# Gathering x1 instead of its normalised form in a decoder layer's experts, with 1/rms entering at the SiLU

## The chip, the cores and the metric

The kernel runs on one core of one Trainium2 chip. The metric is the time of one execution on the device in microseconds (us), lower is better; where runs are compared, the median of several is taken. A profile comes from one profiled execution with its own time. The engines are TensorE (PE in the rows, PEld for its weight loads), VectorE (DVE), ScalarE (ACT), GpSimd (POOL) and SyncE (SP), which issues nearly all transfers here.

## What is computed

One layer of a decoder: 256 tokens of 1024 columns, fp32. First two token mixers, whose gated sum gives x1 = x + merged @ W_out. Then the part that the change touches, a mixture of 32 experts in 4 groups:

```python
h2 = rmsnorm(x1, norm2_g)            # x1 * r * g, r = 1 / rms of the token's row
g_prob = softmax(h2 @ w_rg + b_rg)   # one group of four
e_logits = (h2 @ w_re + b_re)[group] # two experts of the eight in it
hid = silu(h2 @ w1[e]) * (h2 @ w3[e])
out = x1 + sum over the two experts of weight[e] * (hid @ w2[e])
```

Each expert has w1 and w3 of 1024 x 256 and w2 of 256 x 1024. All 32 are read, 96 MB in all.

## The kernel before

**Tiles.** Tokens lie in two tiles of 128 (t = 0, 1). Weights come in chunks of 1 MB (128 x 2048 fp32): 40 for the mixers and W_out ("wf"), then 96 for the experts ("wm"): 8 groups of 4 experts with 12 chunks each, 8 for w1 and w3 (one per 128 input columns, kc = 0 to 7) and 4 for w2. In what follows a "group" is such a group of four experts.

**What sets the order.** All instructions are written out in one order by hand (`manual_schedule`); no scheduler moves them, and each engine runs its own in that order. Chunks lie in slots of SBUF. `Stream.pump` issues the next chunk's transfer on SP's queue as soon as a slot is free, and `done()` frees one after each kc and after each block of y. SP waits in order: the transfer into a slot is issued when the last matmul that reads the slot's old chunk has ended.

**End of the mixers.** `add_x` adds the last products to x and gives x1 in the tile `acc`, with the sum of squares on ScalarE; `rms2` makes r2 = 1/rms on GpSimd; `x1_T` transposes x1, and `logits` multiplies it by the router's weights into `lg`, one bank per token tile.

**The choice** (`choose`, `choice_end`) is a chain of small VectorE steps for each token tile: lg, mx, mi (the group), pen, le, me, ei (the experts), m1, and Mb, a bf16 mask of the two chosen experts; Mf is the same in fp32. `position` multiplies Mb by a triangle of ones on TensorE (for the second tile by ones with the first tile's mask too) to count each token's place in its expert; `pos_m` is that place, masked by Mf. NCH0, NCH1 and NPOS say how the steps of the two tiles alternate. `sel` compares places with 1 to 32: Sg, a matrix of ones and zeros from tokens to 4 x 32 slots.

**res_init(t, half)** puts x1 into the result's bank by a product with the identity and then has ScalarE scale that half of `acc` by r2 in place; the gather below reads the scaled tile under the name h2. Two calls stand ahead of the choice's end, one within it, the fourth behind the first products of group 0.

**A group.** `gather` multiplies x1's (scaled) columns by Sg into `gp` (half 0: kc 0 to 3, half 1: kc 4 to 7), and VectorE evacuates it with the gain g as `hT`. For group 0, `gather0` and `evac0` do half 0 in parts. `products` runs the eight kc into one bank `h`, then SiLU on ScalarE (L1035), the product `hid` on VectorE (L1036), two transpositions `pt`, and four blocks `y` of the second matmul, each copied to `yy` by ScalarE and added into `res` by `comb` with the combination weights. `mids` says which closures run behind which kc: the second half of the gather, `rest` (the combination weights C and the counts of tokens per expert), `back_a` and `back_b` (the matrix SwT for `comb`), and for the next group `sel` behind kc 4 and its gather behind kc 5 and behind the second y. In the last group, `warm` puts filling matmuls `wps` between the products.

Of the kernel before, what the change touches and what calls it, by code (L numbers as in the profile page):

```python
# [15 lines left out]
P = 128  # L16
# [14 lines left out]
LAG_U = (1, 2, 2)  # L31
NCH0, NCH1, NPOS = 2, 6, (5, 6, 7)
PARK = (5, 7)
# [115 lines left out]
def body(tc, cp, sp, tp, mmp, axp, xT_d, xn_d, wf_d, wm_d, wst_d, bs_d, pv_d, rb_d, wr_d, out_d):  # L149
# [554 lines left out]
    Mb = cp.tile([P, NT, 32], BF16, name="Mb")  # L704
    Mf = cp.tile([P, NT, 32], F32, name="Mf")
    C = cp.tile([P, NT, 32], F32, name="C")
# [70 lines left out]
    def res_init(t, half):  # L777

        c = slice(half * 512, half * 512 + 512)
        res[t][half] = mm_ps(f"res{t}{half}")  # L780
        TE.matmul(res[t][half], ident, A["acc"][:, t, c], start=True, stop=True)
        S.activation(A["acc"][:, t, c], A["acc"][:, t, c], AF.Copy, scale=r2[:, t:t + 1])

# [7 lines left out]
    def choose(t):  # L791
# [13 lines left out]
            lambda: V.scalar_tensor_tensor(Mb[:, t], io32, ei[:, 1:2], m1, ALU.is_equal, ALU.add),  # L805
            lambda: V.scalar_tensor_tensor(Mf[:, t], io32, ei[:, 1:2], m1, ALU.is_equal, ALU.add),
        ]

    def position(t):
        pp = ax_ps(f"pos{t}")  # L810
        for s in range(t):
            TE.matmul(pp[:, :32], ones_b, Mb[:, s], start=s == 0, stop=False)
        TE.matmul(pp[:, :32], utri, Mb[:, t], start=t == 0, stop=True)
        return lambda: V.scalar_tensor_tensor(pos_m[:, t], pp[:, :32], 1.0, Mf[:, t], ALU.add, ALU.mult)

    def weights(t):
# [11 lines left out]
        m2 = t1k([P, 32], f"m2_{t}")  # L828
        V.tensor_tensor(m2, Mf[:, t], m1, ALU.subtract)
        V.tensor_scalar_mul(m2, m2, w[:, 3:4])  # L830
# [87 lines left out]
    logits(1, 1)  # L918
    res_init(0, 0)
    res_init(1, 0)  # L920
    h2 = A["acc"]

    def choice_end(sel, gather0, evac0):
# [4 lines left out]
        for i, f in enumerate(ch[1]):  # L928
            f()
            if i < len(rest0):  # L930
                rest0[i]()
            if i == NPOS[0]:
                pm = position(0)
                res_init(0, 1)
            if i == NPOS[1]:
                pm()
            if i == NPOS[2]:
                sel([0])
        pm = position(1)
        for part in range(2):  # L940
            gather0(0, part)
        pm()
# [20 lines left out]
    def group(g, chunks, done, mid, store):  # L963
# [11 lines left out]
        def gather_mm(ps, i, kc, t, start):  # L975
            TE.matmul(ps[:, i * P:(i + 1) * P], h2[:, t, kc * P:(kc + 1) * P], st["S"][:, t].rearrange("p e s -> p (e s)"),  # L976
                      start=start, stop=t == NT - 1, skip_group_check=True)

        def gather_T(hf):
# [7 lines left out]
        def gather(hf):  # L987
            ps = ax_ps(f"gp{g}{hf}")
            for k in range(4):
                for t in range(NT):  # L990
                    gather_mm(ps, k, hf * 4 + k, t, t == 0)
            gather_T(hf)
            gather_out(hf, ps, range(4))

        def gather0(t, part):
# [24 lines left out]
        def products():  # L1020
# [13 lines left out]
            hid = t1k([P, T], f"hid{g}")  # L1034
            S.activation(hid, ps[:, :256], AF.Silu)  # L1035
            V.tensor_tensor(hid, hid, ps[:, 256:], ALU.mult)  # L1036
            pt = ax_ps(f"pt{g}")
# [49 lines left out]
    def run_groups(next_, done_, first, final):  # L1087
# [5 lines left out]
        else:  # L1093
            sel()
            gather(0)
        mids[0][0] = [lambda: res_init(1, 1)] if first else []
        mids[0][1] = [lambda: gather(1)]
        mids[0][2] = [first] if first else []
        mids[0][3] = [back_a]
        mids[0][6] = [back_b]  # L1100
        for g in range(NGRP):
            if g + 1 < NGRP:
                sel_, gather_, back_a_, back_b_ = gr[g + 1][:4]
                mids[g][4] = [sel_]
                mids[g][5] = [lambda ga=gather_: ga(0)]
# [114 lines left out]
```

## Time and profile before

| | before |
|---|---|
| time, median of 3 runs | 468.51 us (467.79 to 469.26) |
| profiled execution: time, span | 468.38 us, 466.7 us |
| TensorE busy | 438.9 us (94% of the span) |
| TensorE weight loads | 334.8 us (72%) |
| VectorE, ScalarE, GpSimd busy | 207.4, 175.3, 94.7 us |
| transfers | 148.80 MB, mean 319 GB/s |
| chain that ended last | PE 81%, DMA 7%, DVE 3%, ACT 3% |

The span runs from the first to the last instruction; the time has some 1.7 us around it. "Busy" is an average over stages with different limits, so it does not say which engine a stage waits for. The chain that ended last is followed back from the last instruction, at each step to what released it, or to the instruction before it on its engine; a share of it is work that the end can be traced to, which need not be work whose removal would move the end. The page's row of transfers by slices of the span shows stretches with little traffic in the mixers and one near the start of the experts' part; behind that it reads 9 tenths and more in each slice but the last.

### The profile page before, as it was taken

How to read it: one execution, taken by the hardware profiler on the slowest of the kernel's cores; microseconds unless marked ns; L12 is line 12 of the kernel's file. 1: busy time of each engine (PE TensorE's matmuls, PEld its weight loads, DVE VectorE, ACT ScalarE, POOL GpSimd, SP SyncE). 2: the span in 40 equal slices, each digit the busy share in tenths (PEclk: the TensorE clock that was granted, in tenths of full speed). 3: DMA queues.
4: the chain of work that ended last, by engine and by line, in shares of the span. 5: the costliest groups of instructions: out<-in, count | busy, mean ns of one | idle time of the engine just before them, and what ended most of it. 6: DMA issues, size and time to landing. Idle time of an engine off the chain costs nothing.

```text
span 466.7 us, 8463 instructions
## 1 busy us (share of the span) xinstructions
PE 438.9 (94%) x3446; PEld 334.8 (72%) x3446; DVE 207.4 (44%) x389; ACT 175.3 (38%) x332; POOL 94.7 (20%) x118
## 2 busy tenths in 40 slices
PE   8989999999999999999999996989898989889984
PEld 6768778878999999999998842645545554636542
DVE  4676576778797655555774643111111011110012
ACT  5747657665665655533444341111000010101001
POOL 1057296456568100004000100000000000000000
PEclk9999999999999999999999998999999999999998
DMA  7999992550227887598767889999999999999992
GB/s 244 344 425 421 416 402 105 180 179 2 93 91 268 322 312 271 213 364 302 310 239 303 315 326 407 422 418 421 406 418 420 421 418 413 412 421 419 422 382 88
DMA packets 27453, 148.80 MB, mean 319 GB/s; under 512 B 3216, under 2 KB 6032, under 8 KB 11152
## 3 DMA queue, kind: packets, MB, share of 16 engines
q1 hardware_dynamic: 27264, 148.18, 80.3%
q8 instruction: 29, 0.48, 0.4%
q14 instruction: 16, 0.13, 0.1%
q10 hardware_dynamic: 144, 0.02, 0.0%
HBM read 147.14 MB, written 1.05 MB: 318 GB/s over the span
## 4 chain that ended last, share of the span: by engine, by line
PE 81%; DMA 7%; DVE 3%; ACT 3%; issue 2%; POOL 1%; SPq 1%; ACTq 0%
PE h L1025 10%; PE y L1067 7%; PE gp L976 6%; PE res L1046 6%; DMA w<-in_wm_dram 4%; DMA xn<-in_xn_dram 2%; PE v L355 2%; PE u L384 2%; PE ga L386 2%; PE b L386 2%; PE b L385 2%; PE b L384 2%; PE a L386 2%; PE a L385 2%; PE a L384 2%
## 5 line engine op out<-in xcount | busy, mean ns | idle before, releaser
L343 DVE TENSOR_TENSOR hl<-w,hl 128x1024 fp32r<-128x1024 f32 (+2 forms) x88 | 90.8, 1036 | 63.3 <-ACT hl L339 61.0
L339 ACT CAST hl<-w 128x1024 fp32r<-128x1024 f32 (+1 forms) x88 | 84.6, 968 | 83.9 <-PE a L386 12.8
L1025 PE MATMUL h<-w,hT 128*32 128x512 f32 x512 | 61.6, 598 | 0.5 <-DMA w<-in_wm_dram 0.4
L984 DVE TENSOR_TENSOR hT<-gp,pv 128x512 f32<-128x512 f32 (+1 forms) x19 | 11.3, 606 | 98.5 <-PE gp L976 98.5
L345 POOL TENSOR_TENSOR hl<-w,hl 128x352 fp32r<-128x352 f32 x32 | 40.5, 1275 | 21.8 <-ACT hl L339 21.7
L1067 PE MATMUL y<-w,hidT 128*32 128x256 f32 (+1 forms) x528 | 34.1, 389 | 4.9 <-issue 4.4
L1073 ACT COPY yy<-y 128x256 f32<-128x256 f32 (+1 forms) x33 | 12.1, 366 | 69.7 <-PE y L1067 69.7
L976 PEld LDWEIGHTS gp<-Sg,acc 128*128 128x128 f32 x256 | 30.4, 192 | 9.2 <-issue 8.0
L1011 POOL TENSOR_TENSOR Sw<-Sg,C 128x128 f32<-128x128 f32 x16 | 6.1, 399 | 151.4 <-PE res L1046 137.0
L1046 PE MATMUL res<-yy,SwT 128*128 128x128 f32 (+1 forms) x192 | 34.8, 323 | 1.1 <-ACT yy L1073 1.0
L1046 PEld LDWEIGHTS res<-yy,SwT 128*128 128x128 f32 x192 | 25.9, 190 | 12.0 <-issue 6.4
L976 PE MATMUL gp<-Sg,acc 128*128 128x128 f32 x256 | 32.0, 278 | 2.1 <-DVE Sg L972 2.1
L1025 PEld LDWEIGHTS h<-w,hT 128*32 128x32 f32 x512 | 13.4, 109 | 24.6 <-issue 19.2
L1067 PEld LDWEIGHTS y<-w,hidT 128*32 128x32 f32 x528 | 16.1, 112 | 17.1 <-issue 9.7
L1035 ACT ACTIVATE hid<-h 128x256 f32<-128x256 f32 x8 | 3.1, 383 | 54.8 <-PE h L1025 54.8
L1036 DVE TENSOR_TENSOR hid<-hid,h 128x256 f32<-128x256 f32 x8 | 3.4, 421 | 35.1 <-ACT hid L1035 35.1
L215 PEld LDWEIGHTS <-ones_b 128*128 128x128 bf16 x205 | 13.2, 106 | 7.8 <-issue 6.7
L384 PE MATMUL u<-xh,hl 128*128 128x256 f32 x64 | 18.8, 293 | 0.0
L384 PE MATMUL ga<-xh,hl 128*128 128x256 f32 x64 | 18.2, 284 | 0.0
L386 PE MATMUL ga<-xh,hl 128*128 128x256 f32 x64 | 18.1, 283 | 0.0
L385 PE MATMUL ga<-xl,hl 128*128 128x256 f32 x64 | 18.1, 283 | 0.0
L384 PE MATMUL gb<-xh,hl 128*128 128x256 f32 x64 | 18.1, 283 | 0.0
(219 smaller groups left out, 957.3 us busy)
## 6 DMA issues: line engine op xcount, KB each, us to landing
w<-in_wm_dram SPq DMA_DIRECT2D x89, 1024.0 KB, 12.6
w<-in_wf_dram SPq DMA_DIRECT2D x36, 1024.0 KB, 11.6
w<-in_wm_dram SPq DMA_DIRECT2D x24, 256.0 KB, 9.1
w<-in_wf_dram SPq DMA_DIRECT2D x8, 256.0 KB, 4.9
w<-in_wf_dram SPq DMA_DIRECT2D x4, 512.0 KB, 8.2
xT<-in_xT_dram SPq DMA_DIRECT2D x8, 128.0 KB, 4.9
xn<-in_xn_dram SPq DMA_DIRECT2D x1, 1024.0 KB, 8.7
xs<-in_xn_dram SPq DMA_DIRECT2D x1, 1024.0 KB, 9.4
```

The lines of the kernel that those rows point to most:

```text
L215: TE.matmul(wps[:, :P], ones_b, ones_b, start=True, stop=True)
L339: S.copy(hl[:, 0, c], raw[:, c])
L343: V.tensor_tensor(hl[:, 1, c.start:m], raw[:, c.start:m], hl[:, 0, c.start:m].bitcast(F32), ALU.subtract)
L345: G.tensor_tensor(hl[:, 1, m:c.stop], raw[:, m:c.stop], hl[:, 0, m:c.stop].bitcast(F32), ALU.subtract)
L384: TE.matmul(o, wh, ah[:, kc], start=kc == 0, stop=False)
L385: TE.matmul(o, wh, al[:, kc], start=False, stop=False)
L386: TE.matmul(o, wl, ah[:, kc], start=False, stop=kc == KC - 1)
L976: TE.matmul(ps[:, i * P:(i + 1) * P], h2[:, t, kc * P:(kc + 1) * P], st["S"][:, t].rearrange("p e s -> p (e s)"), start=start, stop=t == N ...
L1025: TE.matmul(ps[e * SL:(e + 1) * SL], st["h"][kc // 4][:, kc % 4, e * SL:(e + 1) * SL], piece(w, e), start=kc == 0, stop=kc == KC - 1)
L1046: TE.matmul(res[t][c // 512][:, c % 512:c % 512 + n], st["SwT"][:, t * P:(t + 1) * P], yy[:, o:o + n], start=False, stop=True, skip_group_ ...
L1067: TE.matmul(py[e * SL:(e + 1) * SL, :n], hidT[:, f, e * SL:(e + 1) * SL], w[e][:, f], start=f == 0, stop=f == 1)
L1073: S.copy(yy, py[:, :n])
```

## The change

x1 itself is gathered; 1/rms of the tokens is gathered by a product of its own into the slots (`slot_r2`, behind the second half of each group's gather) and enters as ScalarE's scale of the SiLU and in the product of `hid`. `res_init` loses ScalarE's scaling, and all four calls stand behind kc 4 of group 0. Mf goes; Mb is read in its place. NCH1 and NPOS change how the steps of the choice alternate, and the first tile's gather is divided around the second position. In group 0 the second half of the gather moves from behind kc 1 to behind kc 2, and `rest` from behind kc 2 to behind kc 3.

```diff
-NCH0, NCH1, NPOS = 2, 6, (5, 6, 7)
+NCH0, NCH1, NPOS = 2, 8, (1, 3, 4)
...
     def res_init(t, half):
-        c = slice(half * 512, half * 512 + 512)
         res[t][half] = mm_ps(f"res{t}{half}")
-        TE.matmul(res[t][half], ident, A["acc"][:, t, c], start=True, stop=True)
-        S.activation(A["acc"][:, t, c], A["acc"][:, t, c], AF.Copy, scale=r2[:, t:t + 1])
+        TE.matmul(res[t][half], ident, A["acc"][:, t, half * 512:half * 512 + 512], start=True, stop=True)
...
             lambda: V.scalar_tensor_tensor(Mb[:, t], io32, ei[:, 1:2], m1, ALU.is_equal, ALU.add),
-            lambda: V.scalar_tensor_tensor(Mf[:, t], io32, ei[:, 1:2], m1, ALU.is_equal, ALU.add),
...
-        return lambda: V.scalar_tensor_tensor(pos_m[:, t], pp[:, :32], 1.0, Mf[:, t], ALU.add, ALU.mult)
+        return lambda: V.scalar_tensor_tensor(pos_m[:, t], pp[:, :32], 1.0, Mb[:, t], ALU.add, ALU.mult)
...
-    res_init(0, 0)
-    res_init(1, 0)
-    h2 = A["acc"]
+    x1 = A["acc"]
...
             if i == NPOS[0]:
                 pm = position(0)
-                res_init(0, 1)
             if i == NPOS[1]:
                 pm()
             if i == NPOS[2]:
                 sel([0])
+        gather0(0, 0)
         pm = position(1)
-        for part in range(2):
-            gather0(0, part)
+        gather0(0, 1)
         pm()
         sel([1])
...
+        def slot_r2():
+
+            ps = ax_ps(f"r2s{g}")
+            for t in range(NT):
+                TE.matmul(ps[:, :1], st["S"][:, t].rearrange("p e s -> p (e s)"), r2[:, t:t + 1], start=t == 0, stop=t == NT - 1)
+            st["r2"] = tp.tile([P, 1], F32, tag="r2s", name=f"r2s{g}", bufs=2)
+            V.tensor_copy(st["r2"], ps[:, :1])
...
             gather_out(hf, ps, range(4))
+            if hf == 1:
+                slot_r2()
...
-            S.activation(hid, ps[:, :256], AF.Silu)
-            V.tensor_tensor(hid, hid, ps[:, 256:], ALU.mult)
+            S.activation(hid, ps[:, :256], AF.Silu, scale=st["r2"])
+            V.scalar_tensor_tensor(hid, ps[:, 256:], st["r2"], hid, ALU.mult, ALU.mult)
...
-        mids[0][0] = [lambda: res_init(1, 1)] if first else []
-        mids[0][1] = [lambda: gather(1)]
-        mids[0][2] = [first] if first else []
-        mids[0][3] = [back_a]
+        mids[0][2] = [lambda: gather(1)]
+        mids[0][3] = [first, back_a] if first else [back_a]
...
-                mids[g][4] = [sel_]
+                mids[g][4] = [sel_] + [lambda t=t, hf=hf: res_init(t, hf) for t in range(NT) for hf in range(2) if first and g == 0]
```

TensorE between the router's logits and the first products, before (res is the result's bank, the digits behind it the token tile and the half; gp000 and gp001 are the two parts of group 0's gather; ident_152 is the identity):

```order
L781 MATMUL res00_2902<-acc_75_2750,ident_152 128x512
L781 MATMUL res10_2905<-acc_75_2750,ident_152 128x512
L813 LDWEIGHTS utri_168
L813 MATMUL pos0_2923<-Mb_182,utri_168 128x32
L781 MATMUL res01_2925<-acc_75_2750,ident_152 128x512
L812 LDWEIGHTS ones_b_111
L812 MATMUL pos1_2935<-Mb_182,ones_b_111 128x32
L813 LDWEIGHTS utri_168
L813 MATMUL pos1_2935<-Mb_182,utri_168 128x32
L976 MATMUL gp000_2938<-Sg0_2931,acc_75_2750 128x128 x2
L976 MATMUL gp001_2941<-Sg0_2931,acc_75_2750 128x128 x2
```

The same place now:

```order
L809 LDWEIGHTS utri_168
L809 MATMUL pos0_2911<-Mb_182,utri_168 128x32
L969 MATMUL gp000_2923<-Sg0_2917,acc_75_2749 128x128 x2
L808 LDWEIGHTS ones_b_111
L808 MATMUL pos1_2926<-Mb_182,ones_b_111 128x32
L809 LDWEIGHTS utri_168
L809 MATMUL pos1_2926<-Mb_182,utri_168 128x32
L969 MATMUL gp001_2929<-Sg0_2917,acc_75_2749 128x128 x2
```

The three passes with the identity are gone from here, and the first tile's part gp000 stands ahead of the second tile's position.

TensorE behind kc 3 of group 0, before (h0 is the products' bank with the chunk w that each kc reads, gp10 the first half of group 1's gather, pw0 the transposition in `back_b`):

```order
L1025 MATMUL h0_2959<-w_59_2124,hT01_2984 32x512 x4
L1025 MATMUL h0_2959<-w_60_2155,hT01_2984 32x512 x4
L976 MATMUL gp10_3054<-Sg1_3045,acc_75_2750 128x128 x8
L1025 MATMUL h0_2959<-w_61_2215,hT01_2984 32x512 x4
L1016 MATMUL pw0_3071<-ident_152,Sw0_3036 128x128 x2
```

The same place now:

```order
L1028 MATMUL h0_2947<-w_59_2123,hT01_2975 32x512 x4
L779 MATMUL res00_3038<-acc_75_2749,ident_152 128x512
L779 MATMUL res01_3040<-acc_75_2749,ident_152 128x512
L779 MATMUL res10_3042<-acc_75_2749,ident_152 128x512
L779 MATMUL res11_3044<-acc_75_2749,ident_152 128x512
L1028 MATMUL h0_2947<-w_60_2154,hT01_2975 32x512 x4
L969 MATMUL gp10_3052<-Sg1_3035,acc_75_2749 128x128 x8
L1028 MATMUL h0_2947<-w_61_2214,hT01_2975 32x512 x4
```

All four passes stand between kc 4 and kc 5.

VectorE in the choice, before (the digit behind a name is the token tile; Mb, Mf and pos_m hold both tiles):

```order
L796 SCALAR_TENSOR_TENSOR lg1_2875<-lg1_2893,r2_180,rb_2226 128x40
L803 MAX_INDEX ei0_2873<-me0_2872,le_0_2871 128x8
L797 MAX mx1_2876<-lg1_2875 128x8
L804 TENSOR_SCALAR m10_2874<-io32_169,ei0_2873 128x32
L798 MAX_INDEX mi1_2877<-mx1_2876,lg1_2875 128x8
L805 SCALAR_TENSOR_TENSOR Mb_182<-io32_169,ei0_2873,m10_2874 128x32
L799 TENSOR_SCALAR pen1_2878<-io32_169,mi1_2877 128x4
L806 SCALAR_TENSOR_TENSOR Mf_183<-io32_169,ei0_2873,m10_2874 128x32
L800 TENSOR_TENSOR le_1_2879<-lg1_2875,pen1_2878 128x32
L802 MAX me1_2880<-le_1_2879 128x8
```

The same place now:

```order
L800 MAX_INDEX ei0_2872<-me0_2871,le_0_2870 128x8
L801 TENSOR_SCALAR m10_2873<-io32_169,ei0_2872 128x32
L793 SCALAR_TENSOR_TENSOR lg1_2874<-lg1_2892,r2_180,rb_2225 128x40
L802 SCALAR_TENSOR_TENSOR Mb_182<-io32_169,ei0_2872,m10_2873 128x32
L794 MAX mx1_2875<-lg1_2874 128x8
L795 MAX_INDEX mi1_2876<-mx1_2875,lg1_2874 128x8
L796 TENSOR_SCALAR pen1_2877<-io32_169,mi1_2876 128x4
L810 SCALAR_TENSOR_TENSOR pos_m_181<-pos0_2911,Mb_182 128x32
L797 TENSOR_TENSOR le_1_2878<-lg1_2874,pen1_2877 128x32
L965 TENSOR_TENSOR Sg0_2917<-io32p_170,pos_m_181 128x128
L799 MAX me1_2879<-le_1_2878 128x8
```

Tile 0's ei and m stand ahead of tile 1's lg, Mf is gone, and tile 0's place and selection stand further ahead among tile 1's steps.

## Rows read from the trace of the kernel before

**Rows 1.** Chain that ended last, in order of time: start, length, what.

```profile
426.12 20.48 DMA w<-in_wm_dram
```

**Rows 2.** Instructions in order of time, last group: start, length, engine, line [idle before].

```profile
444.16 1.06 PE L1025 MATMUL h<-w,hT 128*32 128x512 f32 x8 [0.19 <-DMA w<-in_wm_dram]
...
446.64 1.07 PE L1025 MATMUL h<-w,hT 128*32 128x512 f32 x8 [0.19 <-DMA w<-in_wm_dram]
...
448.19 0.42 DVE L1036 TENSOR_TENSOR hid<-hid,h 128x256 f32<-128x256 f32 x1 [22.27 <-ACT hid L1035]
449.33 0.39 PE L1039 MATMUL pt<-ident,hid 128*128 128x128 f32 x2
```

**Rows 3.** Busy time by stretch: five engines, then granted clock, DMA share, GB/s.

```profile
272.50:275.00 2.50, 2.50 (x15) 0.60 (x12) 0.00 (x0) 0.96 (x2) 0.00 (x0) 1.00 0.53 156
275.00:446.50 171.50, 156.98 (x1516) 88.60 (x1516) 22.96 (x63) 19.56 (x51) 6.09 (x16) 0.99 1.01 417
```

**Rows 4.** SP's issues of expert chunks in order of time: start, length, count.

```profile
264.50 2.61 SPq L121 DMA_DIRECT2D w<-in_wm_dram  x4
...
272.93 0.33 SPq L123 DMA_DIRECT2D w<-in_wm_dram  x1
...
302.04 0.33 SPq L123 DMA_DIRECT2D w<-in_wm_dram  x1
```

**Rows 5.** The chain that ended last again, from the router to group 1.

```profile
261.20 0.82 PE lg L789 x8
...
267.08 1.79 PE res L781 x4
268.89 0.95 PE res L781 x2
269.99 1.88 PE gp L976 x16
...
272.87 1.05 PE res L781 x2
...
289.85 3.25 PE y L1067 x32
...
312.70 1.93 PE y L1067 x32
```

**Rows 6.** VectorE in order of time, the choice of the second token tile.

```profile
267.19 0.26 DVE L796 SCALAR_TENSOR_TENSOR lg<-lg,r,rb 128x40 f32<-128x40 f32 x1 [0.54 <-PE lg L789]
...
269.51 0.24 DVE L805 SCALAR_TENSOR_TENSOR Mb<-io,ei,m 128x32 bf16<-128x32 f32 x1
...
270.26 0.29 DVE L972 TENSOR_TENSOR Sg<-io32p,pos_m 128x128 f32<-128x128 f32 x1
```

**Rows 7.** All engines in order of time, group 0.

```profile
276.94 0.69 DVE L984 TENSOR_TENSOR hT<-gp,pv 128x512 f32<-128x512 f32 x1 [4.55 <-PE gp L976]
...
277.98 2.78 PE L1025 MATMUL h<-w,hT 128*32 128x512 f32 x24
...
282.39 0.48 DVE L972 TENSOR_TENSOR Sg<-io32p,pos_m 128x128 f32<-128x128 f32 x2
282.82 2.02 PE L976 MATMUL gp<-Sg,acc 128*128 128x128 f32 x16 [2.06 <-DVE Sg L972]
...
288.87 0.46 PE L1039 MATMUL pt<-ident,hid 128*128 128x128 f32 x2 [1.67 <-DVE hid L1036]
```

**Rows 8.** Busy time by stretch, group 0's y and the like place of group 1.

```profile
289.00:292.50 3.50, 2.98 (x30) 1.34 (x34) 0.42 (x1) 0.37 (x1) 0.00 (x0) 0.52 1.03 431
...
310.00:314.00 4.00, 2.35 (x35) 1.17 (x31) 0.85 (x2) 0.55 (x2) 0.00 (x0) 1.00 1.02 424
```

**Rows 9.** ScalarE's groups of instructions by shape: count, busy us, mean ns.

```profile
L448 ACT ACTIVATE qT<-pt_q,gqk 128x512 f32<-128x512 f32 x4 | 2.5, 678 | 0.0
...
L450 ACT COPY kT<-pt_k 128x512 f32<-128x512 f32 x4 | 2.1, 581 | 0.0
```

**Rows 10.** The same view of VectorE.

```profile
L468 DVE SCALAR_TENSOR_TENSOR sc<-dist,sc 128x384 f32<-128x384 f32 x16 | 8.1, 544 | 0.0
```

More of the change, by code (lines that the diff above doesn't have):

```diff
@@ L704, in body @@
     Mb = cp.tile([P, NT, 32], BF16, name="Mb")
-    Mf = cp.tile([P, NT, 32], F32, name="Mf")
     C = cp.tile([P, NT, 32], F32, name="C")
@@ L828, in weights @@
         m2 = t1k([P, 32], f"m2_{t}")
-        V.tensor_tensor(m2, Mf[:, t], m1, ALU.subtract)
+        V.tensor_tensor(m2, Mb[:, t], m1, ALU.subtract)
         V.tensor_scalar_mul(m2, m2, w[:, 3:4])
@@ L975, in gather_mm @@
         def gather_mm(ps, i, kc, t, start):
-            TE.matmul(ps[:, i * P:(i + 1) * P], h2[:, t, kc * P:(kc + 1) * P], st["S"][:, t].rearrange("p e s -> p (e s)"),
+            TE.matmul(ps[:, i * P:(i + 1) * P], x1[:, t, kc * P:(kc + 1) * P], st["S"][:, t].rearrange("p e s -> p (e s)"),
                       start=start, stop=t == NT - 1, skip_group_check=True)
+        def slot_r2():
[4 more added lines that the diff above has]
+            V.tensor_copy(st["r2"], ps[:, :1])
         def gather_T(hf):
```

## The prediction

> **What bounds the kernel now.** I read the end first, then walk back to the place that decides it. The page's chain is four fifths TensorE, but the chain in order of time holds one stretch of 20.48 us, from 426.12 to 446.60, in which the weight transfers came last [rows 1]. Ahead of it the chain only says that TensorE was busy; behind it stands a fixed tail. So the question is since when the transfers run without a gap. The table by stretch answers it: from 275 us to 446.5 the DMA share is 1.01, at 417 GB/s; between 272.5 and 275 it is 0.53 [rows 3]. The queue had run dry because no slot was free: SP issued nothing from 264.50 + 2.61 = 267.11 to 272.93 [rows 4], and then one chunk of 1 MB as soon as the first products of group 0 had read theirs (271.87 to 272.87) [rows 5]. From that issue to a full queue it takes 275.0 - 272.93 = 2.1 us. In the last group the products start 2.48 us apart (444.16, 446.64), one chunk each, the second behind a wait for its transfer [rows 2]. So the end of the kernel is **the first slot that group 0 frees, plus a fixed number of chunks at 2.48 us, plus the tail**.
>
> One more condition: a later slot must not come so late that the queue runs dry again. Counting the issue at 272.93 as the first, the n-th has to come by 272.93 + (n - 1) x 2.48. The thirteenth, the first of group 1, came at 302.04 and was needed by 302.69: 0.65 us to spare [rows 4]. It is the tight one, since eight slots of a group come from its products, four from its y, and all of group 0's work stands ahead of it. What delays group 0 by more than 0.65 us costs time.
>
> **The change, part by part.** *The way to the first products.* Three of the four passes that put x1 into the result stood ahead of them: 1.79 us for two and 0.95 for the third [rows 5]. They lie beside VectorE's choice, though: Mb of the second token tile ends at 269.51 + 0.24 = 269.75 whatever TensorE does, and its position and its selection (270.26 to 270.55) follow from it [rows 6]. Before, the whole gather stood behind that Mb, from 269.99 to 271.87: 0.94 for the first tile, 0.94 for the second [rows 5]. Now half of the first tile's part stands ahead of it, so 0.47 less follows. On VectorE, ei and m of tile 0 now run before lg of tile 1, in what was an idle stretch of 0.54 us [rows 6], and Mf is gone; they partly filled waits between dependent steps, so the gain there lies between 0 and the 0.54; I take 0.15, nearer to nothing, since each step of tile 1 still waits for the one before. Then the second selection ends at 270.40, the first tile's last quarter at 269.99 - 0.15 + 0.47 = 270.31, and the second tile's half runs from 270.40 to 271.34 instead of ending at 271.87: **0.5 us sooner**, between 0.4 (nothing from VectorE: 270.55 + 0.94 = 271.49) and 0.9 (all of it). The gather's wait for ScalarE's scaled x1 goes too; it stood beside Mb and is in this sum. The first issue moves to 272.43.
>
> *Group 0.* All four passes now stand behind its fifth products: 1.79 + 0.95 + 1.05 = 3.79 us, of which 1.05 was in the group already, so +2.74 [rows 5]. The new product that gathers 1/rms by slot is two fp32 matmuls with one moving column. The nearest row is the router's logits, four with 40 columns in 0.82 us [rows 5]: 0.41 us, an upper end; nothing at all, as under the loads beside it, is the lower. I take the upper one. In exchange TensorE's wait of 2.06 us for the second group's selection is covered: between the gather's second half and the second group's gather stand 0.41 of the new product, three products at 2.78 / 3 = 0.93 and the 3.79, together 7.0 us. VectorE needs 5.93 from the start of the evacuation (276.94) to the selection's end (282.87), and the new copy of one column, 0.2 [rows 7]; 0.9 us of cover are left. Sum to the eighth products' end: -0.5 + 2.74 + 0.41 - 2.06 = **+0.6 us**. The sixth and seventh slots are freed later, too, but the seventh, tightest of them, is still in time (the products behind the second group's gather: 282.82 + 2.02 + 1.0 = 285.8 before [rows 7], so 286.4; needed by 272.43 + 14.88 = 287.3). By the thirteenth issue group 1's new product adds 0.41: **+1.0**. The order of the queue's issues is the same as before, and no transfer is added; ScalarE loses four scalings for whose end no one waits later, and its table load for Exp moves up into idle time: nothing.
>
> *The clock.* In the stretch 289 to 292.5 the granted clock was 0.52, the lower of its two levels (1.2 and not 2.4 GHz) for most of it [rows 8], after TensorE had been idle for 2.06 us and then for 1.67 [rows 7]. The first two blocks of y took 3.25 us in it; two blocks of the next group take 1.93 [rows 5]. So 1.3 us of group 0's length hang on that fall. With the 2.06 us filled I take the clock to stay, as it does at the like place of the next group (310 to 314: 1.00) [rows 8]: the thirteenth issue is then 1.0 - 1.3 = -0.3 us against before, and no slot is late.
>
> The Trainium skill (TensorE: Matmul & The Clock Gate, "Why this matters for your kernels") says that a pause between bursts of matmuls can bring the clock down and that dense work holds it up; by that rule the fall goes with the filled pause, and the sum stays the forecast's. The rule speaks as well of the pause of 1.67 us, which stays: if that one is enough, the fall comes back and the second case below holds. No row here shows which of the two pauses brought it.
>
> *All groups.* ScalarE's SiLU takes a column as its scale: evacuations of 512 columns take 678 ns with one and 581 without, so +0.10; VectorE's product becomes a scalar-tensor-tensor, which takes 544 ns for 384 columns, so between 0.36 (by length) and 0.54 for 256 against 0.42 now: -0.06 to +0.12 [rows 2, 9, 10]. In the last group, where it would count, hid is ready at 448.19 + 0.42 = 448.61 and its transposition starts at 449.33, behind TensorE's filling matmuls [rows 2]: 0.72 us of cover for at most 0.22. Without the cover it costs 0.04 to 0.22. Seven more times 0.41 us on TensorE lie under the transfers.
>
> **The rivals.** (a) Forecast: the stream starts 0.5 us sooner and stays fed. The profiled execution took 468.38 us (span 466.7), 0.13 under the median of 468.51; the same step from the median gives **468.0**.
> (b) The clock falls again: then the thirteenth issue is 1.0 us later with 0.65 to spare; the gain is used up and the end moves by +0.35: 468.9. For it: the pause before the transposition stays. Against: the idle 2.06 us ahead of it are gone.
> (c) Slower: VectorE's chain for the combination weights, now behind the evacuation and the new copy, ends later than TensorE's cover, and the wait of 2.06 us stays beside the passes moved in, the clock falling as before. The thirteenth issue is then 1.0 + 2.06 = 3.1 late, the queue dry for 3.1 - 0.65 = 2.4: 470.9. It decides from a delay of 2.1 us (0.65 to spare plus 1.4). Against it: 0.9 us of cover left over.
> (d) The chain's own price: the passes were what the first products waited for, and all 1.79 + 0.95 = 2.74 us come off: 465.8. For it: the chain names TensorE there. Against: VectorE's steps, which end at 270.55 by themselves.
> (e) TensorE decides the end, and the new products cost 7 x 0.41 = 2.9 on it against the 0.5: 470.9. Against: the 20.48 us in which it waited for transfers.
>
> **How the numbers follow.** Chances: (a) 0.60, (b) 0.23, (c) 0.05, (d) 0.06, (e) 0.03, and 0.03 that the start moves without any effect (468.5). A difference of 0.3%, 1.4 us, is about what a measurement of this kernel can tell from no change; (a), (b) and the last lie within it. So faster by more 0.07 ((d) and a little of (a) with a run's spread), within 0.85, slower 0.08. The range: (a) with its ends 0.4 and 0.9 is 467.6 to 468.1, (b) ends at 468.9; the runs shown (467.79 to 469.26) spread by about 0.7 to each side, of which I add 0.6 below and 0.5 above for a median: 467.0 to 469.4. That holds (a), (b) and the case without effect, 0.86, and leaves out (c), (d) and (e).
>
> **What would show it.** Right: SP's first issue of group 0 near 272.4; the DMA share full from 274.5; no idle TensorE before the second group's gather; the clock at 1.00 through 289 to 293; the thirteenth issue before 302.2; the last group's products again every 2.48 us with 0.5 us less in front. Wrong: a DMA share under 0.9 between 290 and 304 is (b) or (c), by whether the clock or the wait for the selection stands in front of it; a first issue before 271 is (d); no wait for transfers before the last group is (e).

## The result and the profile after

The changed kernel takes 475.5 us (median of 4 runs, 474.5 to 479.1) where the kernel before, run beside it, takes 468.65: a ratio of 1.0158, with a 95% interval of 1.0119 to 1.0196. It is **slower by 7 us**; the prediction said 468.0 with 467.0 to 469.4. The profiled execution took 475.41 us with a span of 473.7, against 468.38 and 466.7 before.

The front of the program, up to the router, is the same but for a shift: the choice of the second token tile starts on VectorE at 266.55, 0.64 us sooner than in [rows 6]. I start from there. VectorE's steps in order of time, after:

```profile
266.55 0.26 DVE L793 SCALAR_TENSOR_TENSOR lg<-lg,r,rb 128x40 f32<-128x40 f32 x1
...
268.78 0.25 DVE L802 SCALAR_TENSOR_TENSOR Mb<-io,ei,m 128x32 bf16<-128x32 f32 x1
...
269.53 0.29 DVE L965 TENSOR_TENSOR Sg<-io32p,pos_m 128x128 f32<-128x128 f32 x1
```

From lg to the start of the second selection (Sg) it takes 2.98 us, against 270.26 - 267.19 = 3.07 before [rows 6]. So VectorE's part became a little shorter, as was forecast (0.15). TensorE in order of time, the same place (in brackets its idle time and what ended it):

```profile
267.02 0.18 PE L809 MATMUL pos<-Mb,utri 128*128 128x32 bf16 x1 [0.58 <-DVE Mb L802]
268.21 0.68 PE L969 MATMUL gp<-Sg,acc 128*128 128x128 f32 x4 [1.02 <-DVE me L799]
...
269.09 0.18 PE L809 MATMUL pos<-Mb,utri 128*128 128x32 bf16 x1 [0.17 <-DVE Mb L802]
269.11 2.84 PE L969 MATMUL gp<-Sg,acc 128*128 128x128 f32 x12
271.88 2.48 PE L1028 MATMUL h<-w,hT 128*32 128x512 f32 x16
```

The passes over x1 that had stood here are gone, and nothing fills their place: TensorE waits 0.58 and 1.02 us. Behind these waits twelve products of the gather and 16 of the first hidden products take 2.84 and 2.48 us. The clock is down, as a table by stretch shows (busy time of five engines with counts, then granted clock, DMA share and GB/s):

```profile
270.00:272.00 2.00, 2.00 (x12) 1.78 (x16) 0.50 (x3) 0.00 (x0) 0.00 (x0) 0.50 0.83 291
272.50:275.00 2.50, 2.50 (x24) 0.56 (x16) 0.00 (x0) 0.00 (x0) 0.00 (x0) 0.89 0.28 40
275.00:446.50 171.50, 158.37 (x1448) 90.57 (x1445) 23.89 (x71) 19.16 (x50) 6.12 (x16) 0.97 1.01 417
446.50:452.00 5.50, 5.50 (x79) 3.62 (x76) 0.00 (x0) 0.00 (x0) 0.00 (x0) 1.00 1.00 410
289.00:292.50 3.50, 1.51 (x22) 0.88 (x26) 0.91 (x2) 0.89 (x2) 0.00 (x0) 1.00 0.99 393
313.50:317.50 4.00, 4.00 (x34) 2.36 (x35) 0.00 (x0) 0.74 (x2) 0.00 (x0) 0.57 1.01 424
...
384.00:388.00 4.00, 3.53 (x43) 2.69 (x44) 0.37 (x1) 0.74 (x2) 0.30 (x1) 1.00 1.02 424
```

The first line is the half clock, 0.50 from 270 to 272 (1.2 and not 2.4 GHz). The second has a clock of 0.89 and a DMA share of 0.28 where before had 1.00 and 0.53 [rows 3]: the queue stays dry longer. SP's issues in order of time give the same:

```profile
265.50 1.51 SPq L121 DMA_DIRECT2D w<-in_wm_dram  x1
273.57 1.19 SPq L123 DMA_DIRECT2D w<-in_wm_dram  x2
```

The first issue of group 0 is at 273.57, 7.02 us behind lg, against 272.93 and 5.74 before [rows 4, 6]: 1.28 us later where I had written 0.5 sooner. All that the earlier front gave (0.64) is lost, and 0.64 more.

Group 0 itself, in order of time, all engines:

```profile
277.04 0.50 PE L976 MATMUL r2s<-r,Sg 128*128 128x1 f32 x4
...
279.61 3.70 PE L779 MATMUL res<-acc,ident 128*128 128x512 f32 x8
...
282.75 0.48 DVE L965 TENSOR_TENSOR Sg<-io32p,pos_m 128x128 f32<-128x128 f32 x2
...
284.24 2.05 PE L969 MATMUL gp<-Sg,acc 128*128 128x128 f32 x16
...
290.48 0.44 PE L1042 MATMUL pt<-ident,hid 128*128 128x128 f32 x2 [1.83 <-DVE hid L1039]
```

The gather for group 1 no longer waits for its selection (the 2.06 us of [rows 7] are gone), and the clock is 1.00 from 289 to 292.5 where it was 0.52 [rows 8]. Up to here the forecast holds but for its start. What follows is what it did not see. The chain that ended last, the two blocks of y at the head of the groups, where before had 1.93 in group 1 [rows 5]:

```profile
291.43 1.93 PE y L1070 x32
...
313.46 3.15 PE y L1070 x32
...
337.13 2.93 PE y L1070 x32
...
360.80 2.71 PE y L1070 x32
...
384.47 1.93 PE y L1070 x32
```

In groups 1, 2 and 3 they run at half clock (0.57 over the four microseconds from 313.5 in the table), and the products on res behind them are slow, too: 1.65 us for each of the three. Ahead of each of them TensorE stands and waits for hid. That pause after, in group 1:

```profile
311.34 0.47 ACT L1038 ACTIVATE hid<-h,r2s 128x256 f32<-128x256 f32 x1 [7.06 <-PE h L1028]
311.85 0.48 DVE L1039 SCALAR_TENSOR_TENSOR hid<-h,r2s,hid 128x256 f32<-128x256 f32 x1 [1.75 <-ACT hid L1038]
312.39 0.44 PE L1042 MATMUL pt<-ident,hid 128*128 128x128 f32 x2 [1.17 <-DVE hid L1039]
```

and the same place of the kernel before:

```profile
310.74 0.38 ACT L1035 ACTIVATE hid<-h 128x256 f32<-128x256 f32 x1 [7.07 <-PE h L1025]
311.16 0.42 DVE L1036 TENSOR_TENSOR hid<-hid,h 128x256 f32<-128x256 f32 x1 [1.67 <-ACT hid L1035]
311.63 0.44 PE L1039 MATMUL pt<-ident,hid 128*128 128x128 f32 x2 [1.02 <-DVE hid L1036]
```

SiLU takes 0.47 instead of 0.38 and the multiplication 0.48 instead of 0.42, so that TensorE's pause is 1.17 instead of 1.02.

Last, the end of the chunks. TensorE in order of time, last group, after:

```profile
438.62 1.06 PE L1028 MATMUL h<-w,hT 128*32 128x512 f32 x8
439.62 1.29 PE L215 MATMUL wps<-ones_b 128*128 128x128 bf16 x20
440.84 1.07 PE L1028 MATMUL h<-w,hT 128*32 128x512 f32 x8
...
452.16 1.06 PE L1028 MATMUL h<-w,hT 128*32 128x512 f32 x8
...
454.38 1.07 PE L1028 MATMUL h<-w,hT 128*32 128x512 f32 x8
```

and of the kernel before:

```profile
430.17 1.06 PE L1025 MATMUL h<-w,hT 128*32 128x512 f32 x8
431.16 1.29 PE L215 MATMUL wps<-ones_b 128*128 128x128 bf16 x20
432.38 1.06 PE L1025 MATMUL h<-w,hT 128*32 128x512 f32 x8
...
439.27 1.06 PE L1025 MATMUL h<-w,hT 128*32 128x512 f32 x8
...
441.68 1.07 PE L1025 MATMUL h<-w,hT 128*32 128x512 f32 x8
```

After, every product of the last group follows the one ahead by 2.22 us (452.16 to 454.38), but for one step of 2.44 with two transpositions in it, and no row has a wait for a transfer. 2.22 us is TensorE's own pace: one product (1.0) and the 20 fill products behind it (1.2). Before, the first ones also follow at 2.22 (430.17 to 432.38; 2.45 with the transpositions); only the last three come later than that, by steps of 2.41 (439.27 to 441.68), 2.48 and 2.48, the last two with a wait of 0.19 us for a transfer [rows 2]. So **TensorE paced nearly the whole of the kernel before**, and had some 0.7 us to spare at its end (0.19 + 0.26 + 0.26), not a stretch of 20 us.

The 7 us then add up. The last group's first product is at 438.62 instead of 430.17, +8.45. Of that +0.60 was there at the start of group 1 (301.52 against 300.92). Between them lie six groups of 22.03 instead of 21.54 us, +2.94 (0.34 for the new products of 1/rms, 0.15 for the pause), and three falls of the clock at 1.65, +4.9. 0.7 us of it fill TensorE's spare time: the last product is later by 454.38 - 446.64 = 7.7. Behind it the tail is 0.7 shorter than before (473.7 - 454.38 = 19.3 against 20.1); what remains is 7.0. These 0.7 are no gain of the change: the engines' work in the tail is the same, and the stretch behind the last evacuation, 5.6 here and 6.4 before, lies anywhere between 5.6 and 7.0 in the profiles of the kernels below.

### The profile page after: what moved, and what is told of

Its sections match the earlier page's. It is cut to its first block, busy times and chain, and to the rows that moved or that the text cites. A ratio compares the mean times of both kernels' runs of the same rounds, so it can differ in the third digit from the quotient of the medians.

```text
span 473.7 us, 8518 instructions
## 1 busy us (share of the span) xinstructions
PE 447.2 (94%) x3478; PEld 342.2 (72%) x3478; DVE 209.8 (44%) x395; ACT 173.1 (37%) x328; POOL 92.8 (20%) x118
## 4 chain that ended last, share of the span: by engine, by line
PE 87%; DMA 3%; DVE 2%; ACT 2%; issue 2%; POOL 1%; SPq 1%; ACTq 0%
PE h L1028 12%; PE res L1049 7%; PE y L1070 7%; PE gp L969 6%; PE wps L215 2%; DMA xn<-in_xn_dram 2%; PE v L355 2%; PE u L384 2%; PE b L386 2%; PE b L385 2%; PE b L384 2%; PE a L386 2%; PE a L385 2%; PE a L384 2%; PE gb L386 2%
## 5 line engine op out<-in xcount | busy, mean ns | idle before, releaser
L343 DVE TENSOR_TENSOR hl<-w,hl 128x1024 fp32r<-128x1024 f32 (+2 forms) x88 | 91.9, 1048 | 60.8 <-ACT hl L339 60.2
L1070 PE MATMUL y<-w,hidT 128*32 128x256 f32 (+1 forms) x528 | 35.8, 403 | 4.9 <-issue 4.4
L1049 PE MATMUL res<-yy,SwT 128*128 128x128 f32 (+1 forms) x192 | 36.8, 335 | 1.1 <-ACT yy L1076 1.0
L1049 PEld LDWEIGHTS res<-yy,SwT 128*128 128x128 f32 x192 | 27.2, 198 | 13.5 <-issue 8.4
L969 PE MATMUL gp<-Sg,acc 128*128 128x128 f32 x256 | 33.5, 284 | 1.1 <-DVE me L799 1.0
L1038 ACT ACTIVATE hid<-h,r2s 128x256 f32<-128x256 f32 x8 | 3.8, 474 | 54.1 <-PE h L1028 54.0
L1039 DVE SCALAR_TENSOR_TENSOR hid<-h,r2s,hid 128x256 f32<-128x256 f32 x8 | 3.9, 484 | 35.3 <-ACT hid L1038 35.3
L384 PE MATMUL ga<-xh,hl 128*128 128x256 f32 x64 | 18.2, 284 | 0.0
L384 PE MATMUL gb<-xh,hl 128*128 128x256 f32 x64 | 18.1, 283 | 0.0
L385 PE MATMUL gb<-xl,hl 128*128 128x256 f32 x64 | 18.1, 283 | 0.0
L386 PE MATMUL gb<-xh,hl 128*128 128x256 f32 x64 | 18.1, 283 | 0.0
```

The lines of the kernel that those rows point to most:

```text
L343: V.tensor_tensor(hl[:, 1, c.start:m], raw[:, c.start:m], hl[:, 0, c.start:m].bitcast(F32), ALU.subtract)
L384: TE.matmul(o, wh, ah[:, kc], start=kc == 0, stop=False)
L385: TE.matmul(o, wh, al[:, kc], start=False, stop=False)
L386: TE.matmul(o, wl, ah[:, kc], start=False, stop=kc == KC - 1)
L969: TE.matmul(ps[:, i * P:(i + 1) * P], x1[:, t, kc * P:(kc + 1) * P], st["S"][:, t].rearrange("p e s -> p (e s)"), start=start, stop=t == N ...
L1049: TE.matmul(res[t][c // 512][:, c % 512:c % 512 + n], st["SwT"][:, t * P:(t + 1) * P], yy[:, o:o + n], start=False, stop=True, skip_group_ ...
```

## The experiments

Theory T: TensorE sets the pace, so its work counts in every group. The products of 1/rms cost their length; the columns on SiLU and multiplication cost the clock by a longer pause; the emptied choice costs one more fall of the clock. Rivals S, by run: the moved pieces themselves; something else than the clock behind the columns; the transfers, as the prediction had it. The kernel before took 468.55 us beside the first four runs, 468.71 beside the next four and 467.94 beside the last four.

**Each part alone, on the kernel before.** The products of 1/rms with their copy, unused:

```diff
+            if hf == 1:
+                slot_r2()
```

> The kernel before with the product that gathers 1/rms by slot and its copy added behind each gather's second half; the result is not used. Theory T: seven such products of 0.34 to 0.5 us stand on TensorE ahead of the last group, 2.4 to 3.0 us, of which 0.7 are to spare: 470.3 to 471.0. The prediction's step (they lie under the transfers): 468.6.

Measured: 470.83 us, ratio 1.0038 (0.9994 to 1.0082). The last group's eight products all stand at TensorE's pace now:

```profile
447.54 1.06 PE L1035 MATMUL h<-w,hT 128*32 128x512 f32 x8
449.76 1.06 PE L1035 MATMUL h<-w,hT 128*32 128x512 f32 x8
```

The group takes 21.89 us (311.43 to 333.32 between two transpositions; 21.88 in the next), +0.34; seven times that is 2.4, less 0.7 to spare is 1.7. The span of the profiled execution (470.1) is 3.4 us longer than before (466.7): it has one fall of the clock beside the products, at 357, in a group of 23.87 us, 2.0 more than its neighbours; its groups began 0.7 sooner (first product at 271.10 instead of 271.80); and its tail is 0.3 longer. The prediction's step (nothing, "under the transfers") would have been 468.6. The interval just reaches 1, so the time alone leaves it at "probably"; the pace in the trace is plain.

The column, as one of ones, which changes no value:

```diff
+    one = cp.tile([P, 1], F32, name="one")
+    G.memset(one, 1.0)
...
-            S.activation(hid, ps[:, :256], AF.Silu)
-            V.tensor_tensor(hid, hid, ps[:, 256:], ALU.mult)
+            S.activation(hid, ps[:, :256], AF.Silu, scale=one)
+            V.scalar_tensor_tensor(hid, ps[:, 256:], one, hid, ALU.mult, ALU.mult)
```

> The kernel before with a column of ones as the scale of the SiLU and in the product of hid (scalar-tensor-tensor instead of tensor-tensor); everything else as before. Theory T with the pause as the cause of the falls: each group's pause grows by 0.15 us (1.17 instead of 1.02), by itself 7 x 0.15 - 0.7 = +0.35 us, and the clock falls behind some of the pauses in groups 1 to 6, 1.65 us each: 470 to 475. Theory T with another cause of the falls (the new product, or where group 0 ends): 468.9 and no fall in groups 1 to 6. Rival S: 468.6.

Measured: 473.97 us, ratio 1.0134 (1.0105 to 1.0163). The pause is 1.18, and the chain shows three falls of the clock:

```profile
334.06 1.93 PE y L1069 x32
355.76 2.75 PE y L1069 x32
...
400.80 3.40 PE y L1069 x32
424.14 2.86 PE y L1069 x32
```

A column on two small instructions, 0.15 us of pause a group or 1 us in all, costs 5.4 us (5.3 in the span, 472.0): 1.0 and three times 1.65, less 0.7 to spare, is 5.2. The rest of this execution cancels: group 0 lacks the fall that it has before (1.2 less), the groups began 0.7 later, and the tail is 0.7 longer. To see whether it is the clock, 14 fill products in the pause of each group, on this same kernel:

```diff
-            if store:
-                warm(NW[1])
+            warm(NW[1] if store else 14)
```

> The kernel before with a column of ones as the SiLU's scale and in the multiplication (474.0 without the fill), and 14 fill products in each pause. Theory T (the column's price of 5 us is the clock, which falls behind a pause of 1.17 instead of 1.02 us): no half clock from group 1 on, 468.0 to 469.6. Rival S (the longer pause itself or ScalarE and VectorE behind it cost it): 471 or more.

Measured: 468.04 us, ratio 1.0007 (0.9981 to 1.0033). No group from 1 on falls, and the whole price is gone, with the column still there. So the column's price is the clock.

The third part, order and late passes without the other two, as an edit of the changed kernel (1/rms is left out of the experts, so its values are not those of the layer):

```diff
-            if hf == 1:
-                slot_r2()
...
-            S.activation(hid, ps[:, :256], AF.Silu, scale=st["r2"])
-            V.scalar_tensor_tensor(hid, ps[:, 256:], st["r2"], hid, ALU.mult, ALU.mult)
+            S.activation(hid, ps[:, :256], AF.Silu)
+            V.tensor_tensor(hid, hid, ps[:, 256:], ALU.mult)
```

> The changed kernel without the four r2 products per group and with SiLU and the multiplication as they were before (1/rms is left out of the experts' branch): what is left of the change is the order of the choice, x1 itself in the gather, and the sums' start in group 0's middle. Theory T (TensorE paces the groups, the longer pause before the transposition and the r2 products cost about 7 us between groups 0 and 7, the clock's fall in the choice costs about 1.3 us of TensorE): group period back at 21.5, no half clock in groups 1 to 6, the pause back at 1.02; group 7 starts 0.4 to 1.0 us later than in the kernel before, and the time is 468.4 to 469.9, taken 469.2. Rival S (the moved pieces themselves, that is the order of the choice or the late start of the sums, cost most of the 7 us): above 473. The prediction's own step (stream 0.5 us sooner and nothing else): 467.9.

Measured: 468.72 us, ratio 0.9997 (0.9973 to 1.0022). The clock falls in the choice as in the changed kernel, at 271, the first slot is 7.16 us behind lg, the pauses are back at 1.02 and no group falls. So the reordering can't be told from nothing in the end (the interval is some 1.2 us to each side), and the two things that carry 1/rms cost the 7 us.

**The changed kernel with its pauses filled** (14 products, the same edit as above):

> The changed kernel with 14 small filling matmuls (0.065 us each, 0.9 us in all) on TensorE in the pause between each group's last products and the transposition of hid; nothing else differs. Theory T (TensorE paces the end of the kernel, with about 0.7 us to spare, and in groups 1 to 3 the clock falls behind this pause, 1.65 us each): the falls in groups 1 to 3 go and with them 4.9 us of 475.5, so about 470.6. Rival S (the weight stream decides the end, as I predicted, and it was late or ran dry): TensorE's pace in groups 1 to 6 is of no matter, so 475.5 as before, even where the clock stays.

Measured: 470.67 us, ratio 1.0052 (1.0022 to 1.0082). The pause is down to 0.28, and y runs at full clock in all groups; group 2:

```profile
333.98 0.44 PE L1041 MATMUL pt<-ident,hid 128*128 128x128 f32 x2 [0.28 <-DVE hid L1038]
335.00 1.93 PE L1069 MATMUL y<-w,hidT 128*32 128x256 f32 x32 [0.58 <-DVE hidT L1043]
```

The falls in the groups were 4.8 of the 7 us.

**The changed kernel without the 20 fill products** behind each hidden product:

```diff
-NW = (20, 10)
+NW = (0, 10)
```

> The changed kernel without the 20 filling matmuls behind each product of the last group (8 x 1.22 us of TensorE). Theory T: TensorE is 7.7 us late when it begins the last group and catches up until it meets the transfers' pace of 2.48 us a chunk; the end is then set by the stream, whose first issue stood 0.64 us later in the changed kernel's profile than before: about 469.3, between 468.5 and 470.5. Rival S: the filling lies in waits for transfers, so 475.5, or later where the clock falls.

Measured: 467.89 us, ratio 1.0006 (0.9969 to 1.0043), 1.4 below what T had and under its range. With 1.2 us less of TensorE in each chunk of the last group the transfers decide again, and the products wait for them:

```profile
446.96 1.07 PE L1028 MATMUL h<-w,hT 128*32 128x512 f32 x8 [1.42 <-DMA w<-in_wm_dram]
449.44 1.06 PE L1028 MATMUL h<-w,hT 128*32 128x512 f32 x8 [1.42 <-DMA w<-in_wm_dram]
```

Its profile (an execution of 470.37) has four falls of the clock, in the choice and in groups 0, 5 and 6, and the last chunks still wait for transfers: the falls of groups 5 and 6 lay under the stream. That of group 0 did not: counted as in the prediction, the thirteenth slot came at 303.94 and was needed by 303.24, and between 290 and 310 us the transfers ran at 374 GB/s, against 420 in the kernel before. The same edit on the kernel before is the control:

> The kernel before without the 20 fill products behind each hidden product: TensorE loses 1.3 us of work in each of some 60 chunks. Theory T (in the kernel before the last three chunks already wait for the transfers, so that the stream sets the end and TensorE's spare of 0.7 us is all that the fill uses up): no gain in the end, 467.8 to 469.3, while the last group's hidden products wait 1.2 us or more for transfers. Rival S (TensorE's work sets the end of the kernel before): the end comes by more than 1 us sooner, 467.0 or less.

Measured: 468.01 us, ratio 0.9995 (0.9966 to 1.0024): no gain, as T has it, since the last chunks of the kernel before already waited for transfers. Its last seven hidden products wait for them, 0.6 to 1.4 us each. (The fill stands behind the eight products of the last group alone, not in some 60 chunks.) So in the kernel before the end is set by the stream, as the prediction had it; TensorE was only 0.7 us ahead of it.

**Filling the choice.** In the changed kernel, 6 products ahead of the first positions and 12 behind them:

```diff
             if i == NPOS[0]:
+                warm(6)
                 pm = position(0)
+                warm(12)
```

> The changed kernel with 6 fill products (128x128) ahead of the first positions and 12 behind them in the choice, nothing else. Theory T (TensorE paces everything behind the choice, and the half clock at 269.7 to 273.1 made the first products 1.2 to 1.6 us later): clock 1.00 there, first hidden product and first slot 1.2 to 1.6 us sooner, and all of it arrives at the end: 473.7 to 474.4, if the three falls in later groups stay. Rival S (what happens in the choice is swallowed by a later wait for transfers): 475.5.

Measured: 478.35 us, the median of six from 471.6 to 480.7; the ratio, taken over the three quickest, is 1.0146 (1.0076 to 1.0216): missed, and on the other side. The choice does what T says: clock 1.00 from 266 to 274, the first slot 5.56 us behind lg instead of 7.02. But in the profiled execution (479.28) the clock then falls in six groups in a row, 0 to 5; the chain has five of them:

```profile
313.18 3.49 PE y L1072 x32
...
336.85 3.27 PE y L1072 x32
...
360.52 3.05 PE y L1072 x32
...
384.19 2.83 PE y L1072 x32
...
407.85 2.61 PE y L1072 x32
```

Six times 1.65 is 9.9, against 4.9 in the changed kernel. Its executions go with their mean granted clock: 471.6 us at 0.991, 477 to 481 at 0.972 to 0.981. So a gain of 1.5 us at the front came with more falls behind it, and they cost several times the gain; how many there were in the five executions without a profile is not shown. To take them out of the comparison, the same with the pauses filled as well:

> The changed kernel with fill in both places: 6 and 12 products in the choice, 14 in each pause before the transposition of the hidden values. Theory T (the clock's falls are what made the fill in the choice alone come out at 478; with the pauses filled too, no group falls, and the choice's 1.2 us arrive at the end): 468.8 to 470.2, against 470.7 with the pauses alone filled; what is left over the kernel before are the r2 products on a TensorE that paces the groups (2.22 us between the last group's hidden products, no wait for transfers). Rival S (the fill in the choice is worth nothing or harms by something else): 470.7 or more.

Measured: 469.62 us, ratio 1.0030 (1.0007 to 1.0052), no fall in the profile before the last matmul. (The profiled execution is the longest of the twelve, 472.15, by a front that ends 3 us later.) Against the kernel before run beside it that is 1.7 more: six groups of 21.98 instead of 21.54 us (+2.6), less 0.2 for the first slot and 0.7 to spare. All that the change costs on a steady clock is then little more than the new products, and that is the prediction's rival (e).

Both settings at once, fill in the choice and none behind the products:

> The changed kernel with both: fill in the choice (6 and 12 products) and none behind the hidden products. Theory T (without that fill the transfers set the end again, and then only the stream's start counts; the choice's half clock held the first slot back by 1.2 to 1.6 us): 466.2 to 467.0, against 467.9 for the same kernel without the fill in the choice and 468.5 before. Rival S (the stream's start is not what decides there): 467.9 or more.

Measured: 468.02 us (465.6 to 472.3), ratio 0.9984 (0.9953 to 1.0015): missed in the median, though the profiled execution took 466.12. Its mean clock over the executions is only 0.972 to 0.985; in the profile it falls three times, the last time at 444, in the last group, where nothing covers it. Whether that alone makes the 1.4 us is not settled.

**A mended version and its control.** Both fills, and 12 instead of 20 products behind each hidden product:

> The same with 12 instead of 20 fill products behind each hidden product (4 us less of TensorE in a group). Theory T (TensorE is then ahead of the transfers and keeps its clock, so that the stream sets the end, and its first slot comes about 1.2 us sooner than in the changed kernel): 466.0 to 467.5, the last group's hidden products 2.48 us apart and each waiting for its transfer. Rival S (something that neither TensorE's load nor the stream's start explains holds these kernels at about 468): 467.9 or more, as with the fill in the choice and none behind the hidden products.

Measured: 466.77 us (464.8 to 468.8), ratio 0.9984 (0.9960 to 1.0007). The clock of the profiled execution is 0.998 in the mean, and the last two products wait for their transfers, where T had all eight; the others follow at 1.78 us:

```profile
443.71 1.06 PE L1030 MATMUL h<-w,hT 128*32 128x512 f32 x8 [0.55 <-DMA w<-in_wm_dram]
...
446.19 1.07 PE L1030 MATMUL h<-w,hT 128*32 128x512 f32 x8 [0.64 <-DMA w<-in_wm_dram]
```

The kernel before with the same two settings:

> The kernel before with the same two settings (14 fill products in each pause, 12 behind each hidden product), as the measure for the run ahead. Theory T (the stream sets the end in the kernel before, too, and its start is not touched): 467.5 to 468.6; the changed kernel with the same fills is then sooner by its earlier first slot, 0.5 to 1.5 us. Rival S (the fills alone give the gain, and nothing of it comes from the change): the same time as the run ahead within 0.3 us.

Measured: 467.19 us (465.6 to 470.3), ratio 0.9984 (0.9957 to 1.0012). The two differ by 0.4 us, less than can be told apart here, and not by the 0.5 to 1.5 that I had written. The traces say how much there is to have: the first slot is 5.55 us behind lg with the change and 5.74 without. From that slot to the last hidden product it takes 173.85 us with the change (272.34 to 446.19) and 173.87 without (272.31 to 446.18). So where TensorE keeps its clock and has time to spare, the change is worth some 0.2 us by the traces. Neither version is shown to beat the kernel before; the medians lie 1.2 and 0.8 us under it.

## Why the prediction was wrong

**The step that failed is the reading of the end**: that a stretch of 20.48 us in the chain with "DMA" as its name means that TensorE waits for transfers, and that "seven more times 0.41 us on TensorE lie under the transfers". A chain names one link, here a single transfer from its issue to its landing; it does not say how long the engine at its end stood idle. That stands in the brackets of the timeline: 0.19 us in two places [rows 2], and nowhere ahead of them. I had the two rows 2.48 us apart, and took them for the whole group; most of the products ahead of them stand 2.22 us apart. My own sign of rival (e), no wait for transfers before the last group, held in the kernel before already. The DMA share of 1.01 [rows 3] did not help, since it is full in both kernels. Transfers and TensorE ran almost level, and the change put its weight on the side that had 0.7 us left. The formula itself (first slot, a fixed number of chunks, tail) did hold where the last products wait and the queue stays fed: from the first issue to the last product it takes 173.7 us before and 173.9 in the last two kernels above. In the changed kernel it takes 180.8 (273.57 to 454.38). What was wrong was the cover: 0.7 us of it, where I had counted on enough for seven products. Rival (e) had the mechanism and, with 470.9, nearly the price of the products alone (470.8 on the kernel before, with a fall of the clock in its profile; 469.6 on the changed one with a steady clock), at a chance of 0.03.

**The size of the new products** was nearly right: 0.41 forecast, 0.34 measured.

**The columns** were priced right as instructions and wrong as a pause. Forecast: +0.10 for SiLU, -0.06 to +0.12 for the multiplication; measured: +0.09 and +0.06. The Trainium skill (ScalarE: Activation LUTs, "What ACT_TABLE_LOAD costs") gives some 93 ns for each column operand of an ACTIVATE; the trace agrees, 0.47 against 0.38. But I looked for their cover in the last group alone. In the others TensorE has no fill ahead of the transposition and waits for hid, so the 0.15 us lengthen its idle time; they cost 0.9 us in six groups, and what they do to the clock costs five times as much.

**The clock** was asked about at one place. It did stay up from 289 to 292.5 in the profiled execution, as forecast, and that was in part luck: of the five profiles with this order of group 0 and no fill in its pause, two have y of group 0 at half clock (3.01 us without the 20 fill products, 3.60 with the filled choice). So the pause before the transposition, which stayed, can be enough for it. And two other places were not looked at. In the choice, the passes that I called work "beside VectorE's choice" had kept TensorE busy; without them it idles for 0.58 and 1.02 us, the clock falls, and the start is 1.28 us later instead of 0.5 sooner. The clock falls there in the four profiles of kernels with the emptied choice and in none of the four with fill in it. With fill in their place the gain is there, at 0.2. In the groups, three more falls. The Trainium skill (TensorE: Matmul & The Clock Gate, "HAM oscillation — how this bites in real kernels") describes a kernel whose clock goes up and down with pauses between its matmuls, in every round of its loop; the trace agrees that it goes up and down, but with pauses of 1.17 us, shorter than those of the page's kernel, and not behind each of them: three falls of 1.65 us each in a kernel that is busy otherwise.

**Group 0** came out as its sum said, but for the clock. From the first hidden product to the transposition it takes 290.48 - 271.88 = 18.6 us after and 288.87 - 271.80 = 17.1 before, +1.5; forecast for the eight products were 2.74 + 0.41 - 2.06 = +1.1, and the rest is about the 0.5 that the first 24 products took longer at a falling clock (3.27 us in the chain, against 2.78 for 24 before [rows 7]). The cover for the second selection held: it ends at 283.23, and the gather starts at 284.24.

**The end's spread**: the range had no room for TensorE and clock together, since I had priced each as if the other did not move.

## What to carry over

Before an engine is called idle at the end, read the idle time in front of each of its instructions through the whole last group, not the name of the chain's link: two resources that run level have no cover to give, and then every microsecond on either counts. When a change takes work away from TensorE's front, or makes the instructions that it waits for a little longer, look at what stands in the pause, since the clock's fall behind it may cost many times the pause; a few fill products there are the test and the cure. And where fill keeps the clock up, count it as work of the engine: 20 products behind each chunk of the last group were what put TensorE level with the transfers.

## What the runs showed of the hardware that was not expected

Whether the clock falls behind a pause isn't told by its length alone. With 1.16 to 1.18 us it fell in groups 1, 2 and 3 in the changed kernel, in 3, 5 and 6 with the column of ones, in 1 to 5 with the filled choice (there behind group 0's 1.83 us, too), and in 5 and 6 in the two changed kernels without the 20 fill products: 15 of the 30 such pauses in five profiles. With 1.02 us it fell in none of the groups 1 to 6 in the profiles of three kernels (before, before without the 20, and the order alone), and in one with the products of 1/rms: 1 of 24. With the pause filled (0.29 us or less left) it fell in no group from 1 on in the profiles of five kernels. Nearly every fall costs the same, about 1.65 us of TensorE (2.0 with the products of 1/rms), and where one follows another in successive groups, y mostly takes 0.22 us less each time, and the products behind it more. Why it starts and ends with one group and not another stays open, and so a kernel with such pauses spreads: 471.6 to 480.7 us for one program.
